# Samples' queries queued behind tiles of v, softmax steps one to a page, and squares of two pages reduced together

## The chip, the core and the metric

One Trainium2 chip, one of its cores. The metric is the device time of one launch in microseconds; lower is better. TensorE (PE) multiplies matrices into PSUM, VectorE (DVE) and ScalarE (ACT) read PSUM and the on-chip memory SBUF, GpSimd (POOL) reads SBUF alone, SyncE (SP) issues most transfers. Each engine works through a queue of its own in order and waits on semaphores for the others.

## The reference, cut to what matters

One inference step of a one-layer decoder trunk, with the same weights for a prompt of 512 tokens and for 8 samples of one token each, which attend to 4096 cached positions (32 pages of 128) and to themselves. In `layer`, cut:

```python
z = rmsnorm(x, attn_norm_w) @ w_in          # q_lat, c_kv, k_r, u, v
u, v = gelu(z_u), gelu(z_v)
q = rmsnorm(q_lat) @ w_uq                   # 8 heads of 64 + 32; norms, rope on the 32
attn = attend(...)                          # prompt: causal; samples: pages of the cache
sg = u * (tril(w_s) @ v + b_s)              # spatial gate, chunks of 128 tokens
h = x + concat(attn, sg) @ w_o
h = h + conv_ffn(rmsnorm(h)); h = h + sigmoid(rmsnorm(h) @ w_ple_gate) * e
```

The keys of a cached position are made from its latent row c (128 numbers): for each head `k = rmsnorm(c @ w_uk)`. So a page needs, beside its raw scores, the mean of the squares of 64 numbers for each of its 128 positions and 8 heads; a score is the raw one times the inverse root of that mean, plus the score of the rotated part. Then follow a softmax over 4097 positions and the weighted sum of the rows c.

## The kernel before

All is written in one function, `trunk_step`, with helpers inside it. The program's text gives a priority, not the order: a scheduler at build time fills each engine's queue by when it expects operands to be ready, so an instruction that comes later in the text can be queued earlier. `tc.issue_after(i)` forces what is written under it behind `i` on `i`'s engine.

A float32 product is made of three matmuls (`mm3`, L148 to L151) from a rounded high part and a low part of each operand (`split`, L135): the high part is a cast on ACT (L138, or L140 with a scale), the low part a subtraction, on DVE or on POOL (`sub`, L133; L146).

The stages, in the order of the text:
- The norm of x, the latents, u for four column tiles, q and the prompt's keys per token tile (t = 4 is the 8 samples, t = 0 to 3 are the prompt's 128-token tiles). Norms and rope of q and k (L466 to L477) run on DVE for t = 4, 0, 1 and on POOL for t = 2, 3.
- The samples' queries (L480 to L506): eight transposes on PE (L484), a scale on DVE (L485, `qgT`), the score of a sample with itself on DVE (L486 to L494, `snall`), then the queries folded through `w_ukT` on PE (L500, matmuls of 8 columns) and copied (L502, `qtil`), and the rotated parts copied to `qbd` on ACT (L506). `wukT` lies in a buffer of the three named WR.
- v for token tiles 4, 0, 1, 2, 3 (`v_mm`, 24 matmuls of 512 columns each, and a gelu on ACT, L520), and between them the spatial mixing (`mix`). mix(4) scales the samples' v on DVE (L542, L543), transposes it on PE (L546) and multiplies it with u. mix(t) for the prompt splits v into two tiles of 512 columns (`Q`, three buffers), runs 12 matmuls, adds the bias on DVE (L563) and multiplies with u on POOL (L567) into `sgr`.
- The prompt's attention: `prep_items` transposes q and k of a pair of heads (L645) and splits them; the items of the first pair are interleaved with v. Sixteen blocks of scores, softmax, transposes and sums follow (L662 to L700), with two pages of the first sample in each.
- The samples' pages (`s_page`, 256 of them: 8 samples x 32). A page runs two `mm3` of 260 columns: 256 columns of keys and 4 of raw scores each. ACT squares the keys into a `Q` tile (L761) and copies the raw scores (L762), after which the PSUM tile is free (three of them); DVE sums the squares by head (L763). Pages come in groups of four (n = 0 to 63), whose rows are split on ACT or POOL and POOL (L719, L720 through L133). A gather on POOL (L592) loads the rotated keys, into WR buffers.
- A sample's softmax is done in steps while the next sample's pages run: `steps` holds for a page number (0 to 31 in the sample) what is written after that page. Variance on POOL and Ln on ACT after page 4 (L804, L805), Exp and Square on ACT after 5 (L808, L809), the product with the raw scores after 6 (L815), both instructions of Newton's step after 7 (L160, L161), the sum after 8 (L817), the maximum over pages after 9 (L818), its transpose with page 16 (L794), the maximum over positions and its product with a unit matrix after 17 (L797, L798), the broadcast on PE after 20 (L801), the difference after 21 (L821), Exp after 23 (L781), its sum after 24 (L823), the weighted sum of the rows after 27 (L838, 32 matmuls) and its copy into a `Q` tile after 29 (L847).
- `sgr` is split for the output projection on ACT and POOL after the groups n in `SGS` (L43, L950 to L955). Then come the output projection, the FFN in three thirds, and the gated last part (from about 420 us on; the change does not touch them).

Of the kernel before, what the change touches and what calls it, by code (L numbers as in the profile page):

```python
# [7 lines left out]
F32 = mybir.dt.float32  # L8
# [14 lines left out]
DN = 64  # L23
# [19 lines left out]
SGS = (51, 54, 59, 62)  # L43
# [5 lines left out]
def trunk_step(ctx: ExitStack, tc: tile.TileContext, I, O):  # L49
# [26 lines left out]

    def Q(dt=F32):
        return up.tile([128, 512], dt, tag="sq", name=nm("sq"), bufs=3)
# [403 lines left out]
    ps = ms()  # L482
    for h in range(8):
        nc.tensor.transpose(ps[:96, h * 8:h * 8 + 8], qs_[:8, h * DQ:(h + 1) * DQ], ident[:8, :8])  # L484
    nc.vector.tensor_scalar(qgT.rearrange("p h b -> p (h b)"), ps[:96, 0:64], gq96[:, 0:1], None, op0=ALU.mult)  # L485
    nc.vector.tensor_mul(h96(ks_, 8)[:, :, 0:DN], h96(ks_, 8)[:, :, 0:DN], gqk8[:, 0:1].to_broadcast([8, 8, DN]))  # L486
    nc.vector.tensor_mul(qs_[:8, 0:768], qs_[:8, 0:768], ks_[:8, 0:768])
    snew = S()
    nc.vector.tensor_reduce(snew[:8, 0:8], h96(qs_, 8), axis=AX.X, op=ALU.add)
    nc.vector.tensor_scalar(snew[:8, 0:8], snew[:8, 0:8], SCALE, None, op0=ALU.mult)  # L490
    snall = const([128, 8, 8], F32, "snall")
    nc.gpsimd.memset(snall, NEG)
    nc.vector.tensor_mul(snall[:8], eye8[:, 0].rearrange("p (b h) -> p b h", b=8), snew[:8, 0:8].unsqueeze(1).to_broadcast([8, 8, 8]))
    nc.vector.tensor_add(snall[:8], snall[:8], eye8[:, 1].rearrange("p (b h) -> p b h", b=8))  # L494

    wukT = WR()
    nc.sync.dma_start(wukT[0:64, 0:1024], I["w_ukT"])
    ps = ms()
    for h in range(8):
        nc.tensor.matmul(ps[:, h * 8:h * 8 + 8], wukT[0:64, h * 128:(h + 1) * 128], qgT[0:64, h], start=True, stop=True)  # L500
    qtil = const([128, 8, 8], F32, "qtil")
    nc.vector.tensor_copy(qtil.rearrange("p h b -> p (h b)"), ps[:, 0:64])  # L502
    qbd = const([128, 8, 4, 8], F32, "qbd")
    nc.gpsimd.memset(qbd, 0.0)
    for j in range(4):
        nc.scalar.copy(qbd[32 * j:32 * j + 32, :, j, :], qgT[64:96].rearrange("p h b -> p b h"))  # L506
# [15 lines left out]
    def v_mm(t):  # L522
# [3 lines left out]
        for j in range(4):  # L526
            wh, wl = wget(k_v[j], 3 - j)
            for i in range(2):
                mm3(ps, xh[j][:, i, sl], xl[j][:, i, sl], u3(wh, 2, 512)[:, i], u3(wl, 2, 512)[:, i],
                    j == 0 and i == 0, j == 3 and i == 1)  # L530
# [739 lines left out]
```

## Time and profile before

| | |
|---|---|
| runs timed | 3 |
| median | 905.75 us |
| lowest, highest | 904.86, 906.82 us |
| the profiled execution | 907.9 us, of which the span of instructions is 906.0 us |
| mean granted TensorE clock | 0.989 of full speed |
| PE busy | 884.8 us (98%) |
| DVE, ACT, POOL busy | 645.2, 503.6, 215.0 us |

How to read it: a row of a timeline gives the start, the length, the engine, the line, the operation, out<-in and how many instructions of a kind in succession (x), then in brackets the idle time before it and who ended it. Matmuls are pipelined, so their lengths overlap, and a step from one start to the next says more than a length. The granted clock is the share of full speed that the chip let TensorE run at; a matmul at a lower clock counts as busy for longer. The view of lines gives for a group the busy time, the mean of one in ns and the idle time before.

### The profile page before, as it was taken

How to read it: one execution, taken by the hardware profiler on the slowest of the kernel's cores; microseconds unless marked ns; L12 is line 12 of the kernel's file. 1: busy time of each engine (PE TensorE's matmuls, PEld its weight loads, DVE VectorE, ACT ScalarE, POOL GpSimd, SP SyncE). 2: the span in 40 equal slices, each digit the busy share in tenths (PEclk: the TensorE clock that was granted, in tenths of full speed). 3: DMA queues.
4: the chain of work that ended last, by engine and by line, in shares of the span. 5: the costliest groups of instructions: out<-in, count | busy, mean ns of one | idle time of the engine just before them, and what ended most of it. 6: DMA issues, size and time to landing. Idle time of an engine off the chain costs nothing.

```text
span 906.0 us, 20621 instructions
## 1 busy us (share of the span) xinstructions
PE 884.8 (98%) x7847; PEld 843.4 (93%) x7847; DVE 645.2 (71%) x1093; ACT 503.6 (56%) x1182; POOL 215.0 (24%) x243
## 2 busy tenths in 40 slices
PE   8998999999999999999999999999999999999997
PEld 6896878889999999889999999999999999999997
DVE  6579676668888898796669776337775437766774
ACT  6573368778888888784446443124443224455561
POOL 4004851237777777730000000000000000000000
PEclk9999999999999999999999999999999999999999
DMA  6332160243667664613332222322222322323311
GB/s 220 99 97 82 48 186 1 80 137 98 180 186 214 190 194 135 203 59 110 84 122 88 89 88 75 113 94 94 94 93 71 116 94 83 97 84 100 117 59 60
DMA packets 65347, 100.43 MB, mean 111 GB/s; under 512 B 13841, under 2 KB 47770, under 8 KB 65250
## 3 DMA queue, kind: packets, MB, share of 16 engines
q1 hardware_dynamic: 63202, 94.93, 33.2%
q0 software_dynamic: 2048, 4.20, 1.8%
q8 instruction: 62, 1.02, 0.5%
q14 instruction: 35, 0.29, 0.1%
HBM read 95.95 MB, written 3.15 MB: 109 GB/s over the span
## 4 chain that ended last, share of the span: by engine, by line
PE 77%; DVE 7%; ACT 6%; issue 4%; DMA 3%; SPq 3%; POOL 1%; ACTq 0%; POOLq 0%; DVEq 0%
PE mm L149 23%; PE mm L150 23%; PE mm L151 23%; DVE ss L763 2%; SPq L605 2%; PE ms L838 1%; ACT sq L761 1%; ACT wr L670 1%; PE ms L697 1%; PE ms L149 1%; DMA wr<-w_u 1%; PE ms L151 1%; PE ms L150 1%; DVE wr L673 1%; PE ms L156 1%
## 5 line engine op out<-in xcount | busy, mean ns | idle before, releaser
L149 PE MATMUL mm<-u,w 128*128 128x260 f32 x1392 | 395.2, 284 | 0.1
L151 PE MATMUL mm<-u,w 128*128 128x260 f32 x1392 | 394.7, 284 | 0.0
L150 PE MATMUL mm<-u,w 128*128 128x260 f32 x1392 | 394.1, 283 | 0.0
L150 PEld LDWEIGHTS mm<-u,w 128*128 128x128 f32 x1392 | 263.0, 189 | 0.2
L151 PEld LDWEIGHTS mm<-u,w 128*128 128x128 f32 x1392 | 262.8, 189 | 0.2 <-issue 0.2
L149 PEld LDWEIGHTS mm<-u,w 128*128 128x128 f32 x1392 | 262.5, 189 | 0.5 <-PE mm L151 0.2
L133 DVE TENSOR_TENSOR w<-wr,w 128x1024 fp32r<-128x1024 f32 (+1 forms) x94 | 112.6, 1199 | 106.1 <-issue 54.0
L763 DVE TENSOR_REDUCE ss<-sq 128x8 f32<-128x512 f32 x256 | 166.8, 678 | 26.4 <-ACT sq L761 21.9
L138 ACT CAST w<-wr 128x1024 fp32r<-128x1024 f32 (+1 forms) x94 | 96.5, 1031 | 140.4 <-PE mm L151 127.1
L761 ACT ACTIVATE sq<-mm 128x512 f32<-128x512 f32 x256 | 153.1, 610 | 33.2 <-PE mm L151 18.7
L149 PE MATMUL mm<-wuk,a 128*128 128x260 f32 x416 | 123.4, 297 | 2.5 <-ACT raw L762 2.1
L151 PE MATMUL mm<-wuk,a 128*128 128x260 f32 x416 | 118.4, 285 | 0.0
L150 PE MATMUL mm<-wuk,a 128*128 128x260 f32 x416 | 118.3, 284 | 0.0
L149 PEld LDWEIGHTS mm<-wuk,a 128*128 128x128 f32 x416 | 79.1, 190 | 8.2 <-ACT raw L762 6.3
L150 PEld LDWEIGHTS mm<-wuk,a 128*128 128x128 f32 x416 | 79.1, 190 | 0.0
L151 PEld LDWEIGHTS mm<-wuk,a 128*128 128x128 f32 x416 | 79.0, 190 | 0.0
L592 POOL DMA_INDIRECT wr<-krT,idx x64 | 62.4, 974 | 14.1 <-issue 6.4
L1082 ACT ACTIVATE a<-abuf,cst 128x512 f32<-128x512 f32 x44 | 35.9, 816 | 39.9 <-DVE abuf L1080 38.8
L1083 DVE SCALAR_TENSOR_TENSOR a<-abuf,cst,a 128x512 f32<-128x512 f32 x44 | 33.0, 751 | 25.7 <-ACT a L1082 25.4
L133 POOL TENSOR_TENSOR a<-u,a 128x512 fp32r<-128x512 f32 x34 | 44.2, 1301 | 17.0 <-ACT a L719 15.0
L762 ACT COPY raw<-mm 128x8 f32<-128x8 f32 x256 | 44.5, 174 | 0.0
L138 ACT CAST u<-a 128x520 fp32r<-128x520 f32 x24 | 15.1, 627 | 43.7 <-DVE a L1121 43.3
(307 smaller groups left out, 1324.4 us busy)
## 6 DMA issues: line engine op xcount, KB each, us to landing
wr<-w_ffi SPq DMA_DIRECT2D x44, 512.0 KB
u<-pages SPq DMA_DIRECT2D x152, 128.0 KB
w<-pages SPq DMA_DIRECT2D x104, 128.0 KB
wr<-w_ffo SPq DMA_DIRECT2D x16, 512.0 KB
wr<-w_o SPq DMA_DIRECT2D x8, 512.0 KB
wr<-w_pg SPq DMA_DIRECT2D x8, 512.0 KB
wr<-w_ffo SPq DMA_DIRECT2D x8, 384.0 KB
a<-xT SPq DMA_DIRECT2D x8, 260.0 KB
```

The source lines that it names most:

```text
L133: return (nc.vector if eng == "v" else nc.gpsimd).tensor_sub(dl, src, dh.bitcast(F32))
L138: nc.scalar.copy(dh, src)
L149: nc.tensor.matmul(out, lh, rh, start=start, stop=False)
L150: nc.tensor.matmul(out, lh, rl, start=False, stop=False)
L151: return nc.tensor.matmul(out, ll, rh, start=False, stop=stop)
L592: nc.gpsimd.indirect_dma_start(krT[:, g * 128:(g + 1) * 128], None, I["krT"], bass.IndirectOffsetOnAxis(ap=idx.bitcast(U32)[:, b * 8 + g:b ...
L605: page_dma.append(nc.sync.dma_start(pv[:, j], I["pages"][bass.ds(rs[j], 1)].rearrange("a p f -> (a p) f")))
L761: squares.append(nc.scalar.activation(u3(sq, 2, 256), ps[:, :, 0:256], AF.Square))
L762: nc.scalar.copy(raw[:, c * 8:c * 8 + 8].rearrange("p (a h) -> p a h", a=2), ps[:, :, 256:260])
L763: nc.vector.tensor_reduce(ss[:, c * 8:c * 8 + 8], sq.rearrange("p (h d) -> p h d", d=DN), axis=AX.X, op=ALU.add)
L1082: nc.scalar.activation(c[:, 0:T], a[:, 2:T + 2], AF.Identity, scale=cw[:, m, 2:3], bias=cw[:, m, 3:4])
L1083: nc.vector.scalar_tensor_tensor(c[:, 0:T], a[:, 1:T + 1], cw[:, m, 1:2], c[:, 0:T], op0=ALU.mult, op1=ALU.add)
```

## The change

Four edits, independent of one another:
1. The squares' buffer. `Q` hands out halves of tiles of 1024 columns, of which there are two (before: three tiles of 512). A page with an even number takes a new tile, the odd one its other half, and one reduction over both (128x1024 into 16 columns) follows the odd page. The copy of the weighted sum goes to a `G` tile.
2. The samples' queries are two functions now: `s_queries(after)`, whose transposes are forced behind the last matmul of v's token tile 1 and whose DVE and ACT work comes with it in the text, and `s_folded(after)`, whose matmuls come behind tile 2. The load of `w_ukT` and the two fills stay where they were. The transposes of the prompt's first pair of heads are forced behind tile 3.
3. The steps. Square goes from ACT to DVE as a product (`y0 * y0`), with the product with the raw scores, after page 6; Newton's two instructions after 7 and 8; the sum after 9; the maximum over pages after 10. The product of the maximum with the unit matrix takes a broadcast tensor instead of a scalar operand.
4. `SGS` is (59, 60, 62, 63) instead of (51, 54, 59, 62): all four splits of the gate after groups of the last sample.

```diff
-SGS = (51, 54, 59, 62)
+SGS = (59, 60, 62, 63)
...
+    def QQ(dt=F32):
+        return up.tile([128, 1024], dt, tag="sq", name=nm("sq"), bufs=2)
+    qhalf = {}
     def Q(dt=F32):
-        return up.tile([128, 512], dt, tag="sq", name=nm("sq"), bufs=3)
+        if dt not in qhalf:
+            qhalf[dt] = QQ(dt)
+            return qhalf[dt][:, 0:512]
+        return qhalf.pop(dt)[:, 512:1024]
...
+    def s_queries(after):
+        ps = ms()
+        with tc.issue_after(after.ins):
+            for h in range(8):
+                nc.tensor.transpose(ps[:96, h * 8:h * 8 + 8], qs_[:8, h * DQ:(h + 1) * DQ], ident[:8, :8])
...
+    def s_folded(after):
+        ps = ms()
+        with tc.issue_after(after.ins):
+            for h in range(8):
+                nc.tensor.matmul(ps[:, h * 8:h * 8 + 8], wukT[0:64, h * 128:(h + 1) * 128], qgT[0:64, h], start=True, stop=True)
+        nc.vector.tensor_copy(qtil.rearrange("p h b -> p (h b)"), ps[:, 0:64])
...
-        sq = Q()
+        if j % 2 == 0:
+            bsq["t"] = QQ()
+        sq = bsq["t"][:, j % 2 * 512:j % 2 * 512 + 512]
...
-        nc.vector.tensor_reduce(ss[:, c * 8:c * 8 + 8], sq.rearrange("p (h d) -> p h d", d=DN), axis=AX.X, op=ALU.add)
+        if j % 2:
+            nc.vector.tensor_reduce(ss[:, c * 8 - 8:c * 8 + 8], u3(bsq["t"], 16, DN), axis=AX.X, op=ALU.add)
...
-            nc.vector.tensor_scalar(m2[:8, 8:16], ident[:8, 0:8], m2[:8, 0:1], None, op0=ALU.mult)
+            nc.vector.tensor_mul(m2[:8, 8:16], ident[:8, 0:8], m2[:8, 0:1].to_broadcast([8, 8]))
...
-        def rstd():
-            act(y0, y0, AF.Exp, scale=-0.5)
-            act(t, y0, AF.Square)
+        def square():
+            nc.vector.tensor_mul(t, y0, y0)
+            nc.vector.tensor_mul(raw, raw, y0)
...
-            5: rstd,
-            6: lambda: nc.vector.tensor_mul(raw, raw, y0),
-            7: lambda: newton(raw, ss, raw, t),
-            8: lambda: nc.vector.tensor_add(sc[:, 0:256], sc[:, 0:256], raw),
-            9: lambda: nc.vector.tensor_reduce(m1[:, 0:8], s3.rearrange("p c h -> p h c"), axis=AX.X, op=ALU.max),
+            5: lambda: act(y0, y0, AF.Exp, scale=-0.5),
+            6: square,
+            7: lambda: nc.vector.scalar_tensor_tensor(t, ss, -0.5, t, op0=ALU.mult, op1=ALU.mult),
+            8: lambda: nc.vector.scalar_tensor_tensor(raw, t, 1.5, raw, op0=ALU.add, op1=ALU.mult),
+            9: lambda: nc.vector.tensor_add(sc[:, 0:256], sc[:, 0:256], raw),
+            10: lambda: nc.vector.tensor_reduce(m1[:, 0:8], s3.rearrange("p c h -> p h c"), axis=AX.X, op=ALU.max),
...
     v_mm(0)
     mix(4)
-    p0 = prep_items(0)
-    p0 = prep_items(0)
-    v_mm(1)
+    v1 = v_mm(1)
+    s_queries(v1)
     mix(0)
-    p0[0]()
-    v_mm(2)
+    v2 = v_mm(2)
+    s_folded(v2)
     mix(1)
-    p0[1]()
-    p0[2]()
-    v_mm(3)
+    v3 = v_mm(3)
...
+    p0 = prep_items(0, v3)
+    p0[0]()
+    p0[1]()
     mix(2)
+    p0[2]()
+    p0[3]()
     mix(3)
-    p0[3]()
     p0[4]()
```

More of the change, by code (lines that the diff above doesn't have):

```diff
@@ L481, in trunk_step @@
     qgT = const([96, 8, 8], F32, "qgT")
[L482 to L489, printed above, removed]
@@ L490, in trunk_step @@
[L490 removed]
     snall = const([128, 8, 8], F32, "snall")
+    qtil = const([128, 8, 8], F32, "qtil")
+    qbd = const([128, 8, 4, 8], F32, "qbd")
     nc.gpsimd.memset(snall, NEG)
[L493 to L494 removed]
+    nc.gpsimd.memset(qbd, 0.0)
@@ L496, in trunk_step @@
     wukT = WR()
     nc.sync.dma_start(wukT[0:64, 0:1024], I["w_ukT"])
[L498 to L506, printed above, removed]
+    def s_queries(after):
[3 more added lines that the diff above has]
+                nc.tensor.transpose(ps[:96, h * 8:h * 8 + 8], qs_[:8, h * DQ:(h + 1) * DQ], ident[:8, :8])
+        nc.vector.tensor_scalar(qgT.rearrange("p h b -> p (h b)"), ps[:96, 0:64], gq96[:, 0:1], None, op0=ALU.mult)
+        for j in range(4):
+            nc.scalar.copy(qbd[32 * j:32 * j + 32, :, j, :], qgT[64:96].rearrange("p h b -> p b h"))
+        nc.vector.tensor_mul(h96(ks_, 8)[:, :, 0:DN], h96(ks_, 8)[:, :, 0:DN], gqk8[:, 0:1].to_broadcast([8, 8, DN]))
+        nc.vector.tensor_mul(qs_[:8, 0:768], qs_[:8, 0:768], ks_[:8, 0:768])
+        snew = S()
+        nc.vector.tensor_reduce(snew[:8, 0:8], h96(qs_, 8), axis=AX.X, op=ALU.add)
+        nc.vector.tensor_scalar(snew[:8, 0:8], snew[:8, 0:8], SCALE, None, op0=ALU.mult)
+        nc.vector.tensor_mul(snall[:8], eye8[:, 0].rearrange("p (b h) -> p b h", b=8),
+                             snew[:8, 0:8].unsqueeze(1).to_broadcast([8, 8, 8]))
+        nc.vector.tensor_add(snall[:8], snall[:8], eye8[:, 1].rearrange("p (b h) -> p b h", b=8))
@@ L528, in v_mm @@
             for i in range(2):
-                mm3(ps, xh[j][:, i, sl], xl[j][:, i, sl], u3(wh, 2, 512)[:, i], u3(wl, 2, 512)[:, i],
-                    j == 0 and i == 0, j == 3 and i == 1)
+                last = mm3(ps, xh[j][:, i, sl], xl[j][:, i, sl], u3(wh, 2, 512)[:, i], u3(wl, 2, 512)[:, i],
+                           j == 0 and i == 0, j == 3 and i == 1)
         v_out(t, ps)
+        return last
     def mix(t):
@@ L623, in trunk_step, with prep_items @@
     pq_ = {}
-    def prep_items(hp):
+    def prep_items(hp, after=None):
         qk = [None] * 4
@@ L643, in t_step @@
             ps = ms()
-            for t in range(4):
-                nc.tensor.transpose(ps[:96, t * 128:(t + 1) * 128], src[t][:, h * DQ:(h + 1) * DQ], ident)
+            with ExitStack() as es:
+                if after:
+                    es.enter_context(tc.issue_after(after.ins))
+                for t in range(4):
+                    nc.tensor.transpose(ps[:96, t * 128:(t + 1) * 128], src[t][:, h * DQ:(h + 1) * DQ], ident)
             th, tl = (A(F32R), A(F32R)) if c else (G(F32R), G(F32R))
@@ L705, in trunk_step @@
     bst = {}
+    bsq = {}
     steps, with_qbd = {}, {}
```

2 lines of the change are left out of this document (1 added, 1 removed).

## The prediction

> **What bounds the kernel now.** I read the page first, then the PE engine's waits, then a table by 4 us windows, and then the timelines around the places that these two named. The page's first line of busy times says that TensorE is the engine to follow; L763, the reduction of the squares, is the largest single group of VectorE instructions.
>
> ```profile
> PE 884.8 (98%) x7847; PEld 843.4 (93%) x7847; DVE 645.2 (71%) x1093; ACT 503.6 (56%) x1182; POOL 215.0 (24%) x243
> ```
>
> A 98% busy PE leaves only 906.0 - 884.8 = 21 us of idle, so an edit can pay only by taking away named idle, or a time in which PE was busy at a lower clock. The PE's waits (us in total, times, longest) name the idle that this diff touches:
>
> ```profile
> PE mm L149 <- ACT raw L762: 2.9, 10, 0.8
> PE ms L484 <- DVE u L376: 2.6, 1, 2.6
> PE ms L801 <- DVE s L798: 1.9, 1, 1.9
> ```
>
> L484 are the transposes of the samples' queries, L801 the broadcast of a sample's maximum, and L149 behind L762 a page whose PSUM tile ScalarE had not yet emptied. The windows (columns: PE busy, PEld, DVE, ACT, POOL, granted clock, DMA) show that both large waits cost more than their idle, for the clock behind them falls:
>
> ```profile
> 84.00:88.00 4.00, 1.74 (x12) 1.46 (x13) 4.00 (x12) 0.00 (x0) 4.00 (x2) 0.93 0.00 0
> 88.00:92.00 4.00, 4.00 (x14) 2.95 (x12) 4.00 (x8) 1.90 (x5) 4.00 (x4) 0.64 0.00 0
> 92.00:96.00 4.00, 4.00 (x23) 3.51 (x23) 4.00 (x7) 1.20 (x2) 4.00 (x4) 0.78 0.02 4
> 96.00:100.00 4.00, 4.00 (x16) 3.20 (x15) 4.00 (x7) 1.36 (x4) 4.00 (x4) 0.79 0.00 0
> ...
> 364.00:368.00 4.00, 2.14 (x15) 1.91 (x14) 4.00 (x6) 2.12 (x7) 3.82 (x4) 0.92 0.29 87
> 368.00:372.00 4.00, 4.00 (x25) 4.00 (x25) 2.50 (x5) 2.00 (x7) 0.74 (x3) 0.66 0.69 200
> ```
>
> Three parts of the diff answer to three places: the queries at 84 to 100 us, the maximum at 364 to 372 us, the page loop everywhere between 127 and 408 us. From 420 us on nothing changes.
>
> **Part 1: the samples' queries.** PE's timeline, start and length:
>
> ```profile
> 81.92 0.39 PE L149 MATMUL mm<-w,u 128*128 128x512 f32 x1
> ...
> 83.30 0.40 PE L149 MATMUL mm<-w,u 128*128 128x512 f32 x1
> 86.26 0.54 PE L484 MATMUL ms<-cst,u 8*96 8x8 f32 x8 [2.56 <-DVE u L376]
> ...
> 91.73 1.95 PE L500 MATMUL ms<-qgT,wr 64*128 64x8 f32 x16
> ...
> 101.38 0.41 PE L546 MATMUL ms<-cst,g 8*128 8x8 f32 x4
> ```
>
> Today eight transposes stand in PE's queue after seven matmuls of v's token tile 0, and everything behind them waits 2.56 us for VectorE, though the other matmuls of v need nothing from it. The change puts them behind the last matmul of tile 1. Six matmuls start in 83.30 - 81.92 = 1.38 us, so 0.23 us each, and tiles 0 and 1 (48) end at 81.92 + 48 x 0.23 = 93.0 us without a stall; the queries' data has by then been there for 7 us. Removed: 2.56 us of idle, and of the clock 4 x (0.07 + 0.36) = 1.7 us in the first two windows. The next two lose 4 x (0.22 + 0.21) = 1.7 us; they begin around L500, 1.95 us of narrow matmuls, which the change keeps and puts behind tile 2. I count half of that (0.85) as gained, because the dip needs L500 to fall badly and its place moves; the bounds are nothing and 1.7.
>
> A rule of the Trainium skill would make this term smaller: "TensorE: Matmul & The Clock Gate", section "HAM oscillation — how this bites in real kernels", asks only that PE shows no idle gap over about 3.4 us, so that a gap of 2.56 or 1.9 us would leave the clock alone. By it the clock terms fall away and parts 1 and 2 return idle time alone. The rows with 0.64 behind the one gap and 0.66 behind the other speak against it here.
>
> What is late next is VectorE itself. Its timeline between 84 and 100 us is full in all four windows above, and these are the rows that matter:
>
> ```profile
> 91.94 1.20 DVE L486 TENSOR_TENSOR u<-u,cst 8x512 f32<-8x512 f32 x1
> ...
> 93.41 1.20 DVE L487 TENSOR_TENSOR u<-u,u 8x768 f32<-8x768 f32 x1
> ...
> 94.67 0.93 DVE L489 TENSOR_REDUCE s<-u 8x8 f32<-8x768 f32 x1
> ...
> 96.66 0.70 DVE L490 TENSOR_SCALAR s<-s 8x8 f32<-8x8 f32 x1
> ...
> 97.89 0.75 DVE L493 TENSOR_TENSOR snall<-cst,s 8x64 f32<-8x64 f32 x1
> 98.57 0.96 DVE L543 TENSOR_TENSOR g<-g,cst 8x512 f32<-8x512 f32 x1
> ```
>
> L543 feeds the transposes L546 of the samples' gate, the next thing on PE that needs VectorE. It ends at 99.53 us today. The five operations above it (1.20 + 1.20 + 0.93 + 0.70 + 0.75 = 4.78 us) move behind it, so it ends near 94.75 us. Where L546 will be queued decides: behind tile 1 (93.0 us, about where it stands today) PE waits 1.7 us; half a tile earlier (12 x 0.23 = 2.8 us) 4.5 us; behind tile 2 nothing. I take 1.7 us, and half of a clock dip with it (0.85). Part 1 is then 2.56 + 1.7 + 0.85 - 1.7 - 0.85 = 2.6 us, bounded by 2.56 + 1.7 + 1.7 = 6.0 us above and 4.3 - 4.5 - 1.7 = -1.9 us below.
>
> The prompt's first transposes, moved behind tile 3, are the same instructions later; mix(2) and mix(3) cover the splits of each (one ScalarE and one VectorE instruction on 512 columns), and if that cover is gone an item costs the VectorE one, 0.75 us by the first row below, once or twice. In the same way L506's copies no longer stand in ScalarE's queue before the gelus of v. Queued behind this on POOL and SP: the gathers of the rotated keys (second row) take a buffer that L500 now frees behind tile 2, at about 93.0 + 24 x 0.23 + 1.95 + 1.7 = 102.2 us, which is where they start today; the pages' loads on SP take buffers that tile 3 frees, and come earlier with it. I price both at nothing.
>
> ```profile
> 107.61 0.75 DVE L146 SCALAR_TENSOR_TENSOR g<-ms,gq,g 96x512 fp32r<-96x512 f32 x1
> ...
> 102.16 1.17 POOL L592 DMA_INDIRECT wr<-krT,idx  x1 [0.24 <-issue]
> ```
>
> **Part 2: the sixth sample's maximum.** The chain shows the weighted sums over the pages (L838), one block for each sample, hence the period:
>
> ```profile
> 313.80 1.88 PE ms L838 x64
> 341.86 1.89 PE ms L838 x64
> 374.14 1.88 PE ms L838 x64
> 403.15 1.88 PE ms L838 x64
> ```
>
> 28.06 us in the steady samples, 32.28 us with the wait, 29.01 us after it. In the long one, VectorE against POOL, and the same instruction in a steady sample:
>
> ```profile
> 364.62 2.33 DVE L798 TENSOR_SCALAR s<-cst,s 8x8 f32<-8x8 f32 x1
> ...
> 364.40 1.31 POOL L133 TENSOR_TENSOR u<-u,u 128x520 fp32r<-128x520 f32 x1
> 365.67 1.25 POOL L133 TENSOR_TENSOR a<-u,a 128x512 fp32r<-128x512 f32 x1
> ...
> 251.49 0.21 DVE L798 TENSOR_SCALAR s<-cst,s 8x8 f32<-8x8 f32 x1
> ...
> 250.08 0.98 POOL L592 DMA_INDIRECT wr<-krT,idx  x1
> 251.99 1.28 POOL L133 TENSOR_TENSOR a<-u,a 128x512 fp32r<-128x512 f32 x1 [0.93 <-DMA u<-pages]
> ```
>
> An 8x8 operation that takes 0.21 us takes 2.33 us, and it ends when POOL's two back-to-back subtractions end (365.67 + 1.25 = 366.92). The first of them is the split of the spatial gate (`u<-u,u`, 128x520) which SGS places in this sample. The change moves all four splits to the last sample, so here 32.28 - 28.06 = 4.2 us return; the bounds are 4.2 and nothing (if another POOL instruction meets it). There POOL has room:
>
> ```profile
> 408.09 0.22 POOL L1069 MEMSET abuf<- 128x2 f32 x2 [12.49 <-PE mm L150]
> ```
>
> Four splits of about 1.3 us are 5.2 us in 12.49 us of idle. One of them may meet the seventh sample's maximum for up to 1.3 us; I take 0.4. Part 2 is +3.8 us.
>
> **Part 3: the squares of two pages, and the steps.** By form, a reduction of one page and the nearest one on 1024 elements, and six of them back to back:
>
> ```profile
> L763 DVE TENSOR_REDUCE ss<-sq 128x8 f32<-128x512 f32 x256 | 166.8, 678 | 26.4 <-ACT sq L761 21.9 <-issue 1.4 <-ACT raw L762 0.4
> L667 DVE TENSOR_REDUCE s<-mm 128x2 f32<-128x1024 f32 x4 | 4.8, 1209 | 0.0
> 246.54 3.64 DVE L763 TENSOR_REDUCE ss<-sq 128x8 f32<-128x512 f32 x6
> ```
>
> Two pages cost 2 x 3.64 / 6 = 1.21 us back to back and 2 x 678 = 1356 ns apart; one instruction on 1024 costs 1209 ns. That saves 0 to 0.15 us for a pair, 0 to 2.4 us of VectorE for the 16 pairs of a sample. Against it the square of the estimate moves from ACT to VectorE, and such an operation costs 0.41 us alone and 0.90 us where POOL holds it up:
>
> ```profile
> 241.26 0.90 DVE L815 TENSOR_TENSOR raw<-raw,g 128x256 f32<-128x256 f32 x1
> 244.12 0.41 DVE L161 SCALAR_TENSOR_TENSOR raw<-g,raw 128x256 f32<-128x256 f32 x1
> ```
>
> VectorE is not the bound on average, so what it saves is worth only what PE waits for it: the 2.9 us behind L762 at most, spread over the samples. A first page's squares now wait for the second's, but the buffer holds four halves instead of three. In the last sample, where nothing follows, the pair adds 1209 - 3640/6 = 0.6 us and the square 0.4 us to the chain. I take half of 2.9 less half of 1.0: +1.0 us, bounds -1.0 and +2.9.
>
> **The sum.** 2.6 + 3.8 + 1.0 = 7.4 us. The profiled execution took 907.9 us (span 906.0 us and 1.9 us around it), which makes 900.5 us; it lies 2.15 us above the median of the timed runs, and from that median, 905.75 us, the forecast is 898.4 us.
>
> **The rivals.** (a) PE stalls nowhere new: 6.0 + 4.2 + 2.9 = 13.1 us, 892.7 us. For it speaks that v has 96 matmuls that need no VectorE; against it that VectorE is full from 84 to 100 us. (b) L546 takes L484's place, half a tile early: part 1 becomes -1.9, the sum 2.9, 902.9 us. (c) Slower: the maximum of the steady samples meets POOL. At 251.49 L798 fits between a gather that ends at 251.06 and a subtraction that starts at 251.99, with 0.3 us to spare, and the changed steps shift it. The steady samples repeat one pattern, so it would happen in five of them or none: 5 x 2.1 = 10.5 us at the length of the sixth sample's wait (2.33 - 0.21), 908.9 us with the rest of the sum gained; 919 us with its clock dip too (5 x 4.2). It decides the sign from 7.4 / 5 = 1.5 us a sample, a little over one subtraction of 1.28. The new form of the operation, two tensors instead of a tensor and a scalar, does not protect it: L815 has two tensors and shows 0.90 for 0.41. "GPSIMD Engine Reference", section "Key points", of the Trainium skill lists operations with two inputs in SBUF among those that contend with POOL. Against (c): with one reduction for two pages fewer instructions stand before it. (d) The splits do not go where SGS says: two of today's stand here, before the groups of pages 59 and 62 that name them have begun.
>
> ```profile
> 377.21 2.59 POOL L133 TENSOR_TENSOR u<-u,u 128x520 fp32r<-128x520 f32 x2
> ```
>
> If the four are queued early enough to meet the sixth sample's maximum again, part 2 is nothing and the time 902.2 us.
>
> **How the numbers follow.** Forecast 0.58; (a) 0.17; (b) and (d) together 0.13; (c) 0.12. The range runs from 889.5 us, which is (a) less 3.2 us for waits too short to be listed (of the 21 us of idle the three named here are 7.4), to 905.5 us, the mild end of the others, and leaves out (c) and the far end of (a). A measurement here can tell about 0.2% (1.8 us) from no change. Faster by more than that: 0.58 + 0.17 + 0.10 = 0.85; within it 0.04 (the worse part of (b) and (d) and the mild end of (c)); slower 0.11.
>
> **What would show it.** Right: no wait of L484's transposes in PE's waits, a clock of 1.00 in the windows that follow v's tile 0, L838 blocks 28 us apart in the sixth sample, 128 reductions of 128x1024 near 1.2 us. Wrong: a new PE wait over 1.5 us with a clock below 0.8 behind it (at L546 or in mix(0) for (b)), the multiplication of the maximum at over 1 us in several samples for (c), or `u<-u,u` on POOL beside it for (d).

## The result and the profile after

The changed kernel takes 907.63 us (median of 20 runs, 906.11 to 911.65) against 905.5 us before (20 runs, 902.09 to 907.32): a ratio of 1.0039 with a 95% interval of 1.0028 to 1.0051, so 3.5 us slower (2.5 to 4.6); the medians alone differ by 2.1 us. The forecast was 898.4 us, a gain of 7.4. Of the 20 runs 13 lie between 906.1 and 907.9 us (granted clock 0.992 to 0.994) and 7 between 910.2 and 911.7 (0.988 to 0.992); the profiled one (906.76 us, span 904.5) is of the first group, so the account here explains that group, and what the other runs lose on top, 3.6 us, has no profile.

The two profiles cannot be set side by side from their first microsecond. The first matmul of v starts at 76.38 us before and at 73.81 after, in code that the diff barely touches; in the fifteen kernels of the experiments it starts between 73.2 and 74.8. The profiled execution of before was late in its head by about as much as it lay above its median, 2 us. All spans below are therefore differences between two points of one trace. From the first matmul of v to the end it is 829.64 us before and 830.73 after.

From the page of the changed kernel, the busy time of each engine:

```profile
PE 880.3 (97%) x7847; PEld 839.8 (93%) x7847; DVE 630.3 (70%) x973; ACT 499.7 (55%) x1174; POOL 214.8 (24%) x243
```

VectorE lost 15 us of work (645.2 before), TensorE has the same 7847 instructions, and the time rose all the same. TensorE's waits:

```profile
PE mm L157 <- ACT raw L784: 5.0, 6, 0.9
PE ms L562 <- DVE g L559: 3.8, 1, 3.8
PE mm L157 <- ACT sq L146: 2.1, 1, 2.1
...
PE ms L817 <- DVE s L842: 1.2, 7, 0.3
```

The two waits that the change aimed at (for the queries and for the sixth sample's maximum) are gone. In their place stand one of 3.8 us for the samples' gate, one of 2.1 us for a cast ahead of the first page, and 5.0 instead of 2.9 us for pages whose PSUM tile ScalarE had not emptied. The windows that showed the clock dip before now show a deeper one:

```profile
84.00:88.00 4.00, 4.00 (x18) 3.19 (x17) 4.00 (x11) 0.33 (x1) 4.00 (x1) 1.00 0.00 0
88.00:92.00 4.00, 2.04 (x9) 1.32 (x7) 4.00 (x7) 2.49 (x4) 4.00 (x2) 1.00 0.02 4
92.00:96.00 4.00, 2.12 (x8) 1.35 (x8) 2.20 (x6) 0.00 (x0) 4.00 (x6) 0.73 0.49 133
96.00:100.00 4.00, 4.00 (x23) 3.88 (x23) 2.40 (x4) 3.04 (x7) 3.87 (x6) 0.50 0.00 0
```

The chain of waits between 225 and 425 us (its shares by engine and line, then the blocks of weighted sums that mark the samples) says what the page loop had become:

```profile
by line: DVE ss L786 20.1%; PE mm L157 16.0%; PE mm L158 14.8%; PE mm L159 14.1%; PE ms L862 7.5%; issue 7.1%; ACT sq L783 2.8%; DVE s L842 2.1%; DVE sc L841 1.9%; PE ms L164 1.7%; DVE g L831 1.4%; ACT a L739 1.3%; DVE g L839 1.2%; DVE raw 
...
286.88 1.89 PE ms L862 x64
315.72 1.88 PE ms L862 x64
344.61 1.89 PE ms L862 x64
373.45 1.88 PE ms L862 x64
403.22 1.89 PE ms L862 x64
```

A steady sample takes 28.84 to 28.89 us, where it took 28.06 to 28.14; the sixth, which took 32.28, is now like the others. And the reduction of the squares, VectorE's, holds 20.1% of the chain in this stretch. In the kernel before it holds 5.6%:

```profile
by line: PE mm L149 17.9%; PE mm L150 15.6%; PE mm L151 15.4%; SPq L605 9.5%; issue 7.6%; PE ms L838 6.4%; DVE ss L763 5.6%; ACT sq L761 4.1%; DMA u<-pages 2.3%; PE ms L156 2.1%; SPq L601 1.5%; ACT g L781 1.2%; DVE s L798 1.1%; PE ms L801 1
```

The table cuts each trace at the same points: v (start of its first to start of its last matmul), from there to the first page's first matmul, the stretch with the prompt up to the first sample's weighted sums, the mean of the next four periods, the sixth sample, the seventh, and from the last page's last matmul to the end. All are differences of start times, in us.

| kernel | v | to first page | prompt | steady | sixth | seventh | after last page |
|---|---|---|---|---|---|---|---|
| before | 40.77 | 9.54 | 102.69 | 28.10 | 32.28 | 29.01 | 498.16 |
| changed | 40.67 | 12.47 | 102.09 | 28.88 | 28.84 | 29.77 | 496.66 |
| 1 splits only | 40.63 | 9.23 | 102.71 | 28.10 | 28.13 | 30.01 | 497.30 |
| 2 pairs only | 42.21 | 9.23 | 103.71 | 28.42 | 29.94 | 29.52 | 497.95 |
| 3 steps only | 40.97 | 9.23 | 103.86 | 29.87 | 29.95 | 28.38 | 498.44 |
| 4 queries only | 40.63 | 11.75 | 102.75 | 28.10 | 32.29 | 28.56 | 497.87 |
| 5 steps, square on ScalarE | 40.53 | 9.23 | 102.98 | 28.86 | 29.83 | 28.46 | 498.32 |
| 6 square on VectorE only | 40.48 | 9.24 | 103.81 | 29.75 | 32.10 | 28.46 | 498.38 |
| 7 halves, one reduction a page | 41.90 | 9.24 | 102.94 | 28.09 | 31.92 | 28.50 | 498.06 |
| 9 queries, gate behind tile 2 | 34.91 | 13.28 | 103.86 | 28.11 | 30.79 | 28.53 | 498.15 |
| 12 changed, square on ScalarE | 42.42 | 11.51 | 101.95 | 28.43 | 28.43 | 29.25 | 496.66 |
| 15 changed, square and gate mended | 34.84 | 13.22 | 101.93 | 28.44 | 28.42 | 29.25 | 496.98 |

A row is one execution. The changed kernel and 12 run the same code in v and take 40.67 and 42.42 us there, with a clock of 0.50 for 6.83 us in the one and for 10.24 in the other, so a difference of less than 2 us in that column tells nothing by itself.

For the changed kernel: +2.9 us before the first page, 4 x 0.78 = +3.1 in the steady samples, -3.4 in the sixth, +0.8 in the seventh, -0.7 in v and the prompt's stretch, -1.5 after the last page. That is +1.1 us, beside +1.7 for these 13 runs (907.2 on average, 905.5 before).

### The profile page after: what moved, and what is told of

The parts are those of the page before. It is cut to its first block, busy times and chain, and to the rows that moved or that the text cites. A ratio compares the mean times of both kernels' runs of the same rounds, so it can differ in the third digit from the quotient of the medians.

```text
span 904.5 us, 20370 instructions
## 1 busy us (share of the span) xinstructions
PE 880.3 (97%) x7847; PEld 839.8 (93%) x7847; DVE 630.3 (70%) x973; ACT 499.7 (55%) x1174; POOL 214.8 (24%) x243
## 4 chain that ended last, share of the span: by engine, by line
PE 78%; DVE 11%; ACT 4%; issue 3%; DMA 2%; SPq 1%; POOL 0%; POOLq 0%; DVEq 0%; ACTq 0%
PE mm L157 23%; PE mm L158 23%; PE mm L159 23%; DVE ss L786 5%; PE ms L862 2%; PE ms L716 2%; ACT wr L689 1%; ACT sq L783 1%; PE ms L157 1%; DMA wr<-w_u 1%; PE ms L159 1%; PE ms L158 1%; PE mm L701 1%; PE ms L664 1%; DMA a<-xT 1%
## 5 line engine op out<-in xcount | busy, mean ns | idle before, releaser
L786 DVE TENSOR_REDUCE ss<-sq 128x16 f32<-128x1024 f32 x128 | 155.3, 1214 | 37.2 <-ACT sq L783 36.0
```

Source lines behind the costliest of these rows:

```text
L786: nc.vector.tensor_reduce(ss[:, c * 8 - 8:c * 8 + 8], u3(bsq["t"], 16, DN), axis=AX.X, op=ALU.add)
```

## The experiments

The theory after the result: the splits gave their 4 us; the gate's transposes took the place of the queries' as a stall; and VectorE, 70% busy over the whole span, is full in the second half of a sample, so that the pairs and the square are paid there. The rivals are named with each run. All were timed in five rounds against the kernel before, 1 to 4 on one chip and 5 to 15 on another. Differences are the ratio's distance from 1 times that run's median of before.

### The four parts alone

**1, splits.**

```
-SGS = (51, 54, 59, 62)
+SGS = (59, 60, 62, 63)
```

> The kernel before with the four splits of the spatial gate moved to the last sample, nothing else. Theory A (the trace of after: the sixth sample's period fell from 32.28 us, while its neighbours rose by 0.8): this part is the gain that it was forecast to be, -4.2 us, bounds -3.4 and -4.6, and the steady periods stay at 28.06 us. Rival B (the maximum is held up by some other instruction of POOL once the splits are gone, and only the other edits remove that): -1 to +1 us.

900.98 us, ratio 0.996 (0.9945 to 0.9976): -3.6 us (-5.0 to -2.2). The chain's blocks around the sixth sample are 28.13 us apart:

```profile
339.01 1.88 PE ms L838 x64
367.14 0.65 PE ms L838 x16
```

Theory A. The seventh sample grew by 1.0 us, where 0.4 was allowed for the four splits, and the stretch after the last page shrank by 0.9, which nobody had foreseen.

**2, pairs.** The buffer of two halves and the one reduction (edit 1), nothing else.

> The kernel before with the squares of two pages in halves of one buffer and one reduction for both, nothing else. Theory A (ScalarE's square waits for a buffer that one reduction of 1.21 us frees late, and PE waits for ScalarE): the periods of the samples grow by 0.6 to 1.0 us each, +4 to +6 us in all, and PE waits about 5 us behind the copies of the scores instead of 2.9. Rival B (the growth comes from the steps, the square on VectorE above all): within 1 us of before. The forecast on record: -1 to -2 us.

905.2 us, ratio 1.0013 (1.0001 to 1.0025): +1.2 us (0.1 to 2.3). The steady period is 28.42 us, +0.32: the wait of theory A exists, but at half its size, and the total lies between the two theories.

**3, steps.** The steps on pages of their own, the square on VectorE, the product of two tensors (edit 3), nothing else.

> The kernel before with the softmax steps on pages of their own, the square on VectorE and the maximum's product of two tensors, nothing else. Theory A: 0 to +1 us, most of it the square (0.4 us) in the last sample's chain and the transpose of the maximum, which waits 0.2 us in each sample. Rival B (the steps lengthen each sample): +0.6 to +0.8 us for each of seven samples, +4 to +6 us.

911.09 us, ratio 1.0068 (1.0052 to 1.0083): +6.1 us (4.7 to 7.5). Rival B in kind, and theory A falls: it had put the loss down to the pairs. The steady period is 29.87 us, +1.77, more than twice what B expected. The pairs, which had looked like the culprit, make the steps cheaper: both together give 28.88.

**4, queries.** The queries and folded keys behind tiles 1 and 2, the prompt's first transposes behind tile 3 (edit 2), nothing else.

> The kernel before with the samples' queries behind the tiles of v and the prompt's first transposes behind tile 3, nothing else. Theory A (PE waits 3.8 us for the samples' gate where it waited 2.6 us for the queries, and 2 us more for the cast of mix(3) ahead of the first page): +2 to +4 us, of which 2.9 lie between the last matmul of v and the first page. Rival B (the 2.6 us by which the trace of after reaches v earlier is this edit's and is kept): -1 to +1 us. The forecast on record: -2.6 us.

907.21 us, ratio 1.0027 (1.0016 to 1.0039): +2.4 us (1.4 to 3.5). Theory A: v takes as long as in experiment 1 (40.63 us) though 1.8 us of transposes have left it, and the first page comes 11.75 us after it instead of 9.23, 1.8 of the difference being the transposes themselves.

The four differences add to +6.1 us, the change measures +3.5: they are not independent. With the pairs or the steps alone the sixth sample already exceeds its neighbours by only 1.5 and 0.1 us instead of 4.2, since other instructions then stand beside POOL's.

### What in the steps

**5, the steps with the square left on ScalarE.**

```
+        def rstd():
+            act(y0, y0, AF.Exp, scale=-0.5)
+            act(t, y0, AF.Square)
...
-            5: lambda: act(y0, y0, AF.Exp, scale=-0.5),
-            6: square,
+            5: rstd,
+            6: lambda: nc.vector.tensor_mul(raw, raw, y0),
```

> The kernel before with the softmax steps spread and the maximum's product of two tensors, but the square left on ScalarE behind the exponential. With the steps alone (the third experiment) the steady period was 29.84 us instead of 28.06. Theory A (VectorE's queue is full from the start of these steps to the maximum, so that whatever is put ahead of the maximum is paid by TensorE in full): the square took 0.83 us of that queue, and 0.7 to 1.2 us of the 1.78 go: period 28.6 to 29.1 us, +1 to +4 us in all instead of +7.0. Rival B (the spread itself, the maximum taken a page later, is what costs): period 29.5 us or more, +6 to +7 us. Rival C (the product of two tensors meets POOL wherever it stands): as B, with the product at 0.9 us still.

905.55 us, ratio 1.0012 (0.9999 to 1.0024): +1.1 us (-0.1 to 2.2), period 28.86. Theory A.

**6, the kernel before with only the square on VectorE.**

```
-            act(t, y0, AF.Square)
+        def square():
+            nc.vector.tensor_mul(t, y0, y0)
+            nc.vector.tensor_mul(raw, raw, y0)
...
-            6: lambda: nc.vector.tensor_mul(raw, raw, y0),
+            6: square,
```

> The kernel before with one instruction changed: the square of the estimate is computed by VectorE instead of ScalarE, on the same page as the product behind it; no step is spread. Theory A (VectorE's full queue): the steady period grows by 0.6 to 1.3 us, +3 to +6 us in all, and TensorE waits for the product of the maximum. Rival B (the spread costs, not the square): within 1 us of before, period 28.06 to 28.2 us.

911.7 us, ratio 1.0075 (1.0058 to 1.0092): +6.8 us (5.2 to 8.3), period 29.75. Theory A, beyond its range. One instruction on 128x256, eight times in the program, costs as much as the whole of edit 3. The timeline of the third sample shows how (VectorE, then POOL, then TensorE; start, length):

```profile
268.70 0.90 DVE L811 TENSOR_TENSOR g<-g 128x256 f32<-128x256 f32 x1
...
273.42 1.14 DVE L820 TENSOR_TENSOR sc<-sc,raw 128x256 f32<-128x256 f32 x1
...
275.62 4.23 DVE L763 TENSOR_REDUCE ss<-sq 128x8 f32<-128x512 f32 x7
279.77 0.27 DVE L797 TENSOR_REDUCE s<-ms 8x1 f32<-8x128 f32 x1
279.97 0.66 DVE L763 TENSOR_REDUCE ss<-sq 128x8 f32<-128x512 f32 x1
280.57 0.92 DVE L798 TENSOR_SCALAR s<-cst,s 8x8 f32<-8x8 f32 x1
...
272.98 1.29 POOL L133 TENSOR_TENSOR a<-u,a 128x512 fp32r<-128x512 f32 x1 [1.09 <-ACT a L719]
...
280.19 1.28 POOL L133 TENSOR_TENSOR a<-u,a 128x512 fp32r<-128x512 f32 x1 [1.67 <-ACT a L719]
...
281.54 0.38 PE L801 MATMUL ms<-s,ones 8*128 8x8 f32 x2 [0.81 <-DVE s L798]
```

The square itself (L811) takes 0.90 us, not 0.41. It shifts the sum of scores (L820) into a subtraction of POOL, and that takes 1.14 instead of 0.41. In the built queue seven reductions stand between the column maximum (L821) and the reduction of the maximum (L797), where six did. All of it lands ahead of L797, since VectorE has no gap there. Then the product (L798) meets the next subtraction and ends with it (280.57 + 0.92 = 281.49; 280.19 + 1.28 = 281.47), and TensorE waits 0.81 us. This is the forecast's rival (c), in the third sample's place and at 0.7 us (0.92 - 0.21) instead of 2.1.

The same count was made in every kernel: from the start of a sample's weighted sums to the start of the reduction of the next maximum on VectorE, in the second period.

| kernel | VectorE reaches the maximum after | its idle until then | steady period |
|---|---|---|---|
| 11 product on POOL | 20.43 | 2.99 | 27.85 |
| before | 20.66 | 2.81 | 28.10 |
| 7 halves, one reduction a page | 20.68 | 2.82 | 28.09 |
| 2 pairs | 21.03 | 3.96 | 28.42 |
| 12 changed, square on ScalarE | 21.03 | 3.96 | 28.43 |
| changed | 21.61 | 3.97 | 28.88 |
| 5 steps, square on ScalarE | 21.71 | 2.84 | 28.86 |
| 6 square on VectorE | 22.89 | 2.57 | 29.75 |
| 3 steps | 22.90 | 2.58 | 29.87 |

Over these kernels each microsecond by which VectorE is late at the maximum goes with about 0.75 us of the period ((29.75 - 28.10) / (22.89 - 20.66) = 0.74). Where TensorE pays it differs. In this period its longest wait is at the broadcast of the maximum in 3 and 6 (0.92 and 0.81 us), and with the pairs at a page that waits for ScalarE's copy (0.53 us in 2 and 12, 0.84 in the changed kernel), some 5 us ahead of the maximum; in 5 no wait is longer than 0.16 us. And the pairs do not make VectorE fuller: it idles 1.15 us longer than before and is still 0.37 us later. In experiment 5 it is one instruction: the sum of scores meets POOL and holds VectorE 1.39 us instead of 0.33 (+1.06, and the maximum is reached 1.05 later).

**11, the counter-test.** Splits as in 1, and the product of scores and estimate on POOL.

```
-            6: lambda: nc.vector.tensor_mul(raw, raw, y0),
+            6: lambda: nc.gpsimd.tensor_mul(raw, raw, y0),
```

> The first experiment (splits in the last sample, -3.1 us), and the product of the scores with the estimate computed by POOL instead of VectorE: 0.83 us a sample less in VectorE's queue ahead of the maximum, the counter-test to the square that was added there. Theory A (what VectorE has ahead of the maximum is paid by TensorE): the steady period falls from 28.06 us to 27.4 to 27.8, -5 to -7 us in all. Rival B (28.06 is set by TensorE and ScalarE, and only an excess over it counts): period 28.0 to 28.1 us, -3 us. Rival C (the product on POOL holds up VectorE's instructions of two inputs or delays the pages' subtractions): period over 28.3 us, -1 us or slower.

901.32 us, ratio 0.9968 (0.9954 to 0.9983): -2.9 us, no better than experiment 1. The steady period fell to 27.85 us, between what A and B expected: there is only a quarter of a microsecond to be had, and TensorE is then idle for 0.16 us of the second period (0.24 before). What it brings is lost in the prompt's stretch (105.13 us for 102.71) and the seventh sample (30.52).

### What in the pairs

**7, the buffer of halves with a reduction for each page.**

```
-        if j % 2:
-            nc.vector.tensor_reduce(ss[:, c * 8 - 8:c * 8 + 8], u3(bsq["t"], 16, DN), axis=AX.X, op=ALU.add)
+        nc.vector.tensor_reduce(ss[:, c * 8:c * 8 + 8], sq.rearrange("p (h d) -> p h d", d=DN), axis=AX.X, op=ALU.add)
```

> The kernel before with the buffer of two halves that is freed as a whole, but a reduction for each page as before, so that only the buffer's form differs. With pairs alone (the second experiment) the steady period was 28.43 us instead of 28.06 and TensorE waited 0.69 us between the 17th and 18th page of a sample. Theory A (the wait comes of the buffer, which is freed two pages at a time and only when the second reduction has ended): the period stays at 28.4 us or grows to 28.8, since two reductions of 0.61 us take as long as one of 1.21. Rival B (the length of the one instruction is what ScalarE waits for): the wait goes and the period is 28.06 us again.

904.78 us, ratio 0.9996 (0.9982 to 1.0009), steady period 28.09: rival B. The buffer's form alone costs nothing; the long instruction on it does. In the changed kernel's timeline (VectorE, POOL, ScalarE, TensorE) the whole wait can be read:

```profile
270.27 0.42 DVE L831 TENSOR_TENSOR g<-g 128x256 f32<-128x256 f32 x1
270.60 1.54 DVE L832 TENSOR_TENSOR raw<-raw,g 128x256 f32<-128x256 f32 x1
272.06 1.21 DVE L786 TENSOR_REDUCE ss<-sq 128x16 f32<-128x1024 f32 x1
...
270.43 1.42 POOL L141 TENSOR_TENSOR a<-u,a 128x512 fp32r<-128x512 f32 x1
...
273.36 0.60 ACT L783 ACTIVATE sq<-mm 128x512 f32<-128x512 f32 x1 [1.61 <-DVE ss L786]
...
274.06 0.39 PE L157 MATMUL mm<-wuk,a 128*128 128x260 f32 x1 [0.84 <-ACT raw L784]
```

Two products stand ahead of a reduction of 1.21 us, one of them held to 1.54 us by POOL's subtraction; ScalarE has filled both tiles and waits 1.61 us for the first to come free; TensorE, its PSUM tiles full, waits 0.84. With 0.6 us reductions a buffer would have come free halfway. The meeting with POOL is not the square's doing: in experiment 12, without it, the next product meets the same subtraction (L839, 1.53 us), and TensorE waits 0.53. What the square adds is an instruction of 0.42 us ahead of the reduction. A third tile of two pages does not fit into SBUF and was not tried.

**12, the changed kernel with the square back on ScalarE** (the edit of experiment 5).

> The changed kernel with one thing undone: the square is left on ScalarE behind the exponential. The changed kernel's steady period is 28.87 us and its time +3.5 us. Theory A (the square's 0.33 to 0.41 us in VectorE's queue are paid in each sample): period 28.4 to 28.5 us as with the pairs alone, -2.5 to -4 us against the changed kernel, 0 to +1 us against before. Rival B (the one reduction of 1.2 us alone makes TensorE wait once a sample, and with it VectorE has room for the square): period 28.8 to 28.9 us, +3 us against before.

903.35 us, ratio 0.9988 (0.9973 to 1.0003): -1.1 us against before (-2.4 to +0.3), and 0.0051 x 905 = 4.6 us better than the changed kernel. Theory A, a little beyond both its ranges; the period is 28.43, that of the pairs alone.

### What in the queries

**8, the prompt's first transposes as before.** Experiment 4 with `p0[0]()` to `p0[2]()` between the tiles of v again, without the order behind tile 3.

> The kernel before with the samples' queries behind tile 1 and the folded keys behind tile 2, but the prompt's first transposes left between the tiles of v as before. The queries with the transposes moved (the fourth experiment) were +3.1 us, with 11.75 us between the last matmul of v and the first page instead of 9.2 to 9.5. Theory A (the transposes behind tile 3 are what costs: mix(3)'s cast waits in ScalarE's queue, and the cover that was assumed is not there): 9.2 to 9.6 us there, within 1 us of before in all, since the stall for the samples' gate takes the place of the stall for the queries. Rival B (the folded keys free the gathers' buffer later, and the first pages wait for that): 11 us or more there still, +2 to +3 us in all.

907.04 us, ratio 1.0026 (1.0012 to 1.0040): +2.4 us, as in 4. Theory A falls: moving the transposes cost nothing. They are 1.8 us of TensorE's time (three groups of 0.60) that leave v and come back behind it. In 8 they stand in v, which takes 42.29 us; the first page is still 11.33 us behind it. Both numbers are rival B's. TensorE waits 0.7 us there for the load of `w_uv`, and the clock stands at 0.50 from 122.13 to 125.55 us. The cause that rival B named is in the trace too: POOL's gathers start only at 109.05 us, after a wait of 3.6 us for the folded keys (L512), and ScalarE's copy of the prompt's values waits 5.0 us for POOL's products behind them. No run separates the two.

**9, the samples' gate behind tile 2.** Experiment 4, and its transposes are taken out of `mix(4)`:

```
+    def s_gate(mx, after):
+        ps = ms()
+        with tc.issue_after(after.ins):
+            for gp in range(4):
+                nc.tensor.transpose(ps[:, gp * 8:gp * 8 + 8], mx[:8, gp * 128:(gp + 1) * 128], ident[:8, :8])
...
     s_folded(v2)
+    s_gate(mx4, v2)
```

> The queries' part of the change alone, with one more move: the transposes of the samples' gate are queued behind tile 2 as well, not ahead of the last three matmuls of tile 1. Without that move the part was +3.1 us and TensorE waited 3.9 us for the gate. Theory A (that wait takes the place of the one for the queries and costs as much or more): it goes, the clock behind it stays at 1.00, v's stage from its first to its last matmul shrinks from 40.6 us to 35 to 37, and the total comes to -1 to -3 us. Rival B (VectorE is so full here that the next thing which needs it is late instead, the cast and subtraction for mix(0)): v's stage at 38 us or more, the total at 0 to +3 us.

904.38 us, ratio 0.9997 (0.9983 to 1.0012): -0.3 us against before (-1.5 to +1.1), 2.7 better than 4. In v theory A holds to the letter, 34.91 us, and the clock stays up; in the total it does not.

```profile
88.00:92.00 4.00, 4.00 (x23) 2.89 (x21) 4.00 (x7) 2.82 (x4) 4.00 (x2) 1.00 0.02 4
92.00:96.00 4.00, 3.18 (x19) 2.79 (x19) 3.97 (x6) 1.17 (x3) 4.00 (x3) 1.00 0.43 133
96.00:100.00 4.00, 4.00 (x18) 2.95 (x17) 2.09 (x5) 1.93 (x5) 3.92 (x8) 1.00 0.00 0
```

But of the 5.7 us against experiment 1, 4.0 go again before the first page, 1.8 for the moved transposes and 2.1 for this wait (POOL, ScalarE, TensorE), and 1.1 in the prompt's stretch, where the clock falls to 0.50 behind the wait:

```profile
118.36 3.34 POOL L578 TENSOR_TENSOR u<-g,a 128x128 f32<-128x128 f32 x8
...
120.08 0.59 ACT L648 COPY g<-ms 128x512 f32<-128x512 f32 x1 [4.56 <-POOL u L578]
...
120.72 1.00 PE L659 MATMUL ms<-cst,u 128*96 128x128 f32 x6 [2.14 <-ACT g L648]
```

ScalarE's copy of the prompt's values needs a buffer that POOL's products of the mix free, and those stand in POOL's queue behind gathers and a page's split.

**10, splits and mended queries together.**

> The ninth experiment with the four splits in the last sample as in the first: the two parts touch different stages, so their differences add. If theory A of the ninth holds: -4 to -6 us; under its rival: -3 to 0 us.

900.25 us, ratio 0.9955 (0.9937 to 0.9973): -4.1 us (-5.7 to -2.4). The parts add, 3.6 and 0.3.

**13 and 14, the products of the mix for tokens 256 to 511 on VectorE,** in experiments 10 and 1.

```
-            nc.gpsimd.tensor_mul(sgr[gp // 2][:, gp % 2, t0:t0 + n], mv[:, gp], uT[gp][:, t0:t0 + n])
+            (nc.vector if t > 1 else nc.gpsimd).tensor_mul(sgr[gp // 2][:, gp % 2, t0:t0 + n], mv[:, gp], uT[gp][:, t0:t0 + n])
```

> The tenth experiment (splits moved, queries and gate behind the tiles of v), and the products of the spatial mix for tokens 256 to 511 computed by VectorE instead of POOL. In the ninth, v's stage was 5.7 us shorter than with the queries alone made late, but 13.3 us instead of 9.2 passed from its last matmul to the first page, 1.8 of them the transposes that moved there, and ScalarE's copy of the prompt's values ended 4.6 us late behind POOL's products. Theory A (POOL, full from 100 to 120 us with gathers one behind the other, is what the prompt's first blocks then wait for): the wait for that copy goes, 10.5 to 11.3 us to the first page, -5 to -6.5 us in all. Rival B (ScalarE's casts behind its table load, and the moved transposes, set the first page): 12 us or more still, -4 us in all.

> The control for the thirteenth: the first experiment (splits moved, -3.1 us) with the same products on VectorE, queries and transposes as in the kernel before. Theory A: with v's stage at its old length nothing on TensorE's path waits for POOL there, so -2.5 to -4 us, 9.2 to 9.5 us from v to the first page. Rival B (POOL is late in the kernel before as well): the first page comes 1 us or more earlier, -4 to -5 us.

13: 901.79 us, ratio 0.9971 (0.9961 to 0.9981), -2.6 us. 14: 902.44 us, ratio 0.9972 (0.9963 to 0.9982), -2.5 us. Neither theory foresaw this. In 13 the copy no longer waits for POOL, yet the first page comes 16.58 us after v instead of 12.09, because VectorE is now what is late:

```profile
PE mm L151 <- DVE sq L133: 3.0, 2, 2.1
...
PE ms L659 <- DVE g L146: 2.1, 3, 1.5
```

The control loses 1.1 us to experiment 1, its first page 11.57 us after v instead of 9.23. So the wait on POOL was real, but taking the work off POOL does not show what the stretch would be without it; that stays open.

**15, the changed kernel with the gate behind tile 2 and the square on ScalarE.**

> The changed kernel with two things mended: the transposes of the samples' gate behind tile 2, and the square on ScalarE. The square alone, mended, gave -1.1 us against the kernel before. Theory A (the two are separate causes in separate stages, and what remains against the kernel before is the splits' gain less the pairs' 0.36 us a sample and 1 us in the last one): v's stage at 35 to 37 us, periods at 28.4 us, -2.5 to -4.5 us. Rival B (what is gained in v is given back before the first page): -0.5 to -2 us.

898.62 us, ratio 0.9936 (0.9922 to 0.9950): -5.8 us (-7.1 to -4.5), more than theory A's range, and the fastest kernel of the study. Its granted clock is 0.997 or 0.998 in all six runs, where the 20 of before show 0.989 to 0.996; that may be what the theory left out. The places of the square and of the gate's transposes separate +3.5 from -5.8 us: by the ratios 4.6 us for the square (12) and 4.7 for the gate (15 less 12).

## Why the prediction was wrong

**What bounds the kernel: half right.** "VectorE is not the bound on average, so what it saves is worth only what PE waits for it" is true of the average, 71%. The step that failed is taking this share for the page loop. There VectorE has 2.8 us idle in the 20.66 us up to the maximum, all of it early (none in the last 9.4 us), and a delay there goes with a longer period at three quarters (the table with experiment 6). The profile of before held the sign: L798 and L801 were the costliest wait of the sixth sample, and the steady samples passed POOL's subtraction with 0.3 us to spare.

**Part 1: wrong, in where L546 would be queued and in when VectorE would be ready for it.** The text had the rule ("Where L546 will be queued decides") and three prices; it took "behind tile 1 ... PE waits 1.7 us". The scheduler queued it (now L562) ahead of tile 1's last three matmuls, 0.7 us early. And VectorE finished L559 (L543 before) 20.0 us after v's first matmul, where 94.75 - 76.38 = 18.4 were forecast. One of the five operations that were to "move behind it", L507 (L486 before), still stands ahead, and L559 takes 1.52 us beside POOL instead of 0.96 (VectorE, POOL, TensorE):

```profile
88.18 1.52 DVE L507 TENSOR_TENSOR u<-u,cst 8x512 f32<-8x512 f32 x1
...
92.30 1.52 DVE L559 TENSOR_TENSOR g<-g,cst 8x512 f32<-8x512 f32 x1
...
89.12 4.16 POOL L480 TENSOR_TENSOR u<-u,g 128x512 f32<-128x512 f32 x1
...
93.88 0.59 PE L562 MATMUL ms<-cst,g 8*128 8x8 f32 x4 [3.84 <-DVE g L559]
```

So the wait is 3.84 us for the 1.7 taken, and the clock gave nothing back: it stands at 0.50 for 6.83 us in both profiles. That is rival (b) in kind. Its price for this part, -1.9 us, is near the -2.4 that the part alone measured, but it had L546 half a tile early and VectorE on time, so the size is partly luck. Experiment 9 confirms the other end too: with the gate behind tile 2 v is 5.7 us shorter, 3.9 without the transposes that left it, between the +2.6 taken and the bound of 6.0. But "I price both at nothing" fell for the stretch behind v. The transposes' own 1.8 us do move without a loss (experiment 8), as forecast; the gathers, forecast "at about ... 102.2 us, which is where they start today", start at 107.97 in a trace that reaches v 2.57 us earlier, after a wait of 3.55 us for the folded matmuls, and most of what the mended kernel gains in v is lost there again, to a buffer that POOL frees late and to the clock.

**Part 2: right.** 4.2 us forecast for the sixth sample, 4.15 measured in experiment 1. Some 1.5 us of that were the clock behind the wait, which does not fall in every execution (last section). "I take 0.4" for a split that meets the seventh sample should have been 1.0. "From 420 us on nothing changes" missed 0.9 us. The sum, +3.8, measured 3.6.

**Part 3: wrong in sign.** "I take half of 2.9 less half of 1.0: +1.0 us, bounds -1.0 and +2.9"; alone, the pairs lose 1.2 and the steps 6.1 us. Two steps of the working failed. "The buffer holds four halves instead of three" counted capacity; what decides is how long ScalarE waits for the next half, and that grew with the reduction from 0.6 to 1.21 us (experiments 2 and 7). And the square was charged only "in the last sample, where nothing follows", 0.4 us; it is paid in every sample, 0.45 us with the pairs ((28.88 - 28.43), experiment 12) and 1.65 without (experiment 6). In the last sample, on the other hand, the longer chain costs nothing: behind the last page TensorE passes 85 matmuls of the output projection ahead of the next stage where it passed 71, so the 1.35 us by which the last weighted sums come later are filled with work that was due anyway.

**The rivals.** (c) had the right sign, slower in every steady sample, with too small a chance and for one mechanism only, the maximum meeting POOL. That mechanism shows in experiments 3 and 6, where the product takes 0.91 and 0.92 us. In the changed kernel its product is short (0.14 us), and the loss is TensorE's wait for a buffer of squares, 0.84 us, with the square ahead of the reduction. The condition should have been "VectorE is later in the second half of a sample", whatever delays it.

## What to carry to other kernels

Before giving an engine an instruction, ask how full it is in the stretch where the instruction lands and whether anything waits at the end of that stretch; a share over the whole span answers neither, and a count of the engine's idle time up to what the other engine waits for does (none in the last 9.4 us here); the chain of waits cut to the stretch confirms it afterwards (5.6% for a line before, 20.1% after). When a stall is moved out of a queue, look up what the scheduler will put into the place that comes free: the next instruction with the same late producer takes the stall over, unless it is ordered back too. One long instruction instead of two short ones saves its engine time and still loses if another engine waits for the buffer that the first short one would have freed.

## What was new about the hardware

The clock and the length of a gap. The same code waits for the sixth sample's maximum for 1.86 us until 367.00 us in the kernel before and for 1.87 us until 363.79 in experiment 9 (columns as in the windows above, before first):

```profile
363.92:367.33 3.41, 1.55 (x14) 1.32 (x12) 3.41 (x4) 2.20 (x8) 3.23 (x4) 1.00 0.21 60
367.33:370.74 3.41, 3.41 (x17) 3.41 (x17) 2.42 (x5) 1.07 (x3) 0.71 (x1) 0.50 0.65 186
...
360.24:363.65 3.41, 1.68 (x14) 1.47 (x13) 3.41 (x4) 2.67 (x9) 3.39 (x3) 1.00 0.14 30
363.65:367.06 3.41, 3.27 (x26) 3.25 (x27) 3.35 (x7) 1.77 (x5) 1.57 (x3) 1.00 0.71 203
```

Behind the one the clock falls and the sample takes 32.28 us, behind the other it stays and the sample takes 30.79. These windows are the trace's own: the clock of every trace here is 1.00 or 0.50 and changes only at the borders of stretches of 3.41 us, which lie elsewhere in each execution; values between are mixtures. Between 40 and 880 us of the 17 traces the clock fell behind all 13 stretches in which TensorE was busy for less than 40%, behind 7 of 14 with 45 to 58%, and behind 15 of over 4000 busier ones, each of which holds eight or more matmuls of 8 columns (the queries and folded keys). So the length of a gap alone does not decide; how it falls on these stretches counts, and above 58% only stretches with narrow matmuls lost the clock, though not all of them did. In the changed kernel TensorE idles 2.14 us until 119.31 us, across the border at 117.75, and the clock stays; in experiment 9 it idles 2.14 us until 120.72, within the stretch that ends at 121.30, and the clock falls. The gap there also follows 32 narrow matmuls (32 columns each) instead of full ones, and no run separates the two. "TensorE: Matmul & The Clock Gate" of the Trainium skill, section "HAM oscillation — how this bites in real kernels", asks for a gap of over about 3.4 us; by that none of these four gaps should lower the clock, and two do, while the gap of 3.84 us at L562 (clock 0.73, then 0.50) agrees with it.

An operation of VectorE that met POOL was held in both forms seen: 8x8 of a tensor and a scalar 0.92 us instead of 0.21 (L798 in experiment 6), 128x256 of two tensors 1.54 instead of 0.41 (L832). The reductions, which read one tensor, kept their length beside it: 0.66 us at 279.97 in experiment 6, where POOL's subtraction starts at 280.19.

The stretch after the last page takes 496.7 to 497.3 us in the eight kernels with the splits in the last sample and 497.9 to 498.4 in the nine without: 400 matmuls in a row take 47.96 and 48.12 us. Why the place of four splits changes the pace of matmuls 100 us later was not tried.
